# Two cuts of x moved one product ahead, and another first transfer on ScalarE's queue

## The chip, the cores and the metric

The kernel runs on one core of one Trainium2 chip. The metric is the device time of one execution in microseconds (us), as the median of the runs shown. A profiled execution gives, beside its own time, the trace that is read below.

## The reference

One encoder layer works on 512 tokens of width 1024, all in float32:

```python
x = x + FFN_RES * _swiglu(_rmsnorm(x, norm_ffn1[l]), w_ffn1_gu[l], w_ffn1_down[l])
h = _rmsnorm(x, norm_mix[l])
xr, gr, q, k, v, ga, gb = jnp.split(h @ w_in[l], splits, axis=-1)
...
x = x + y @ w_out[l]
x = x + FFN_RES * _swiglu(_rmsnorm(x, norm_ffn2[l]), w_ffn2_gu[l], w_ffn2_down[l])
```

`_swiglu` multiplies by a 1024 x 5632 matrix, takes silu of the first half of the columns times the second half, and multiplies by a 2816 x 1024 matrix. Between the two feed-forward networks stand a gated recurrence and a neighbourhood attention. The change touches the first feed-forward network (FFN) alone, and in it the first product, and one small scaling of a constant later on.

## The kernel before, in words

**Precision.** Every float32 operand that TensorE multiplies is split in two: a high part H, made by a copy on ScalarE (`split`, L140), and a low part L, the rest, made by a subtraction on VectorE (L143). A product is then three matmuls: H by H, L by H and H by L. In the rows that follow `wh` and `wl` are the parts of a weight, `xh` and `xl` those of x. A weight's tile is 128 x 1024 and is cut into four pairs of buffers in turn, so the cut of one tile waits until TensorE is done with the tile four before it.

**The lead.** x arrives in eight tiles of 128 x 512, two to a `pair` tile. With each goes a tile of the first weight `w1gu` (`wraw`), the plain part of the first FFN's columns. All of these transfers are issued on SyncE's queue, but for the first weight tile, which is issued on ScalarE's queue (L457), behind `small`, a 128 x 114 tile of constants (L123). For each x tile ScalarE makes the high part scaled by a column of `small` (L191), the square (L197, L200) and a copy scaled by the norm's weight, `xg` (L670).

**The Strassen stage.** The other columns of the first FFN go by one level of Strassen's scheme, in five units of 512 columns of each half (`strassen`, a variant of it with seven products). The seven products of a unit are called `a11`, `a12`, `s1`, `s2`, `s4`, `s3` and `a22` after the form of x that each takes: quarters of x, or one of four sums of quarters. Those sums, the *forms* s1, s2, s4 and s3, are made once and used by all units: `raw` makes each out of `xg` on VectorE (L258 and L256, in halves of 128 x 256), and `cut` splits it in H and L (128 x 512 tiles named `s` in the rows). Each form has two such tiles, so two cuts. `need(n)` in `strassen` says where in the program form n is cut: before, `need("s4")` stands behind product s2, and `need("s3")` behind product s4. A product is 24 matmuls of 128 x 512, in two halves of twelve; each half has one tile of weights and one tile of the form.

**Sums of weights.** Four of a unit's seven products take sums of weight blocks. Some are made by VectorE (`sums`, L340: `pair` plus a `PT` or `wraw` tile, 128 x 1024), some by a transfer that adds (`add`, L335, on GpSimd's queue). Product a11 of unit one, the second unit, is begun early, between s1 and the rest of unit zero. Its later product s1 takes `pair` + `PT`, two sums on VectorE (`pair_523 + PT_735` and `pair_525 + PT_737`).

**What sets the order.** Each engine runs its instructions in one order, fixed when the kernel is built. A scheduler forms it from the program's order, priorities and expected readiness; `after(i, prev)` holds i behind prev in that order without a wait on the chip. So a step that waits holds back all that is queued behind it on its engine. `ready` (L506 to L515) prepares the plain part's hidden tiles (`pre`) once the first norm is known, `plus` (L353) adds a product to a kept one, `put` (L374, L376) makes and turns a hidden tile, and `evict` (L348) copies a product out.

Of the kernel before, what the change touches and what calls it, by code (L numbers as in the profile page):

```python
# [11 lines left out]
AF = mybir.ActivationFunctionType  # L12
ALU = mybir.AluOpType
# [10 lines left out]
HD = 64  # L24
# [19 lines left out]
C_QN, C_KN = 112, 113  # L44
# [42 lines left out]
def block_kernel(ctx: ExitStack, tc, a, out):  # L87
    nc = tc.nc
# [12 lines left out]
    mark = {}  # L101
# [18 lines left out]


    small = const.tile([P, NSMALL], F32, name="small")
    nc.scalar.dma_start(small, a["small"])  # L123
    xd = dram.tile([KT, P, T], F32, name="xd")
    vd = [dram.tile([ROWS, GW, T], F32, name=nm("vd")) for _ in range(2)]
    xres = [None] * KT
# [2 lines left out]
    ones = const.tile([P, P], F32, name="ones")  # L129
# [2 lines left out]
    for _ in range(NWARM):  # L132
        nc.tensor.matmul(aux_t()[:, :P], ones, ones, start=True, stop=True)
    warm = const.tile([P, 1], F32, name="warm")
    nc.scalar.activation(warm, ones[:, 0:1], AF.Sqrt)


    def split(raw, H, L, act=True):
# [42 lines left out]
    def make_xg(gcol, tag):  # L181
        xh, xl = [], []
        for k in range(KT):
            xh.append(xpool.tile([P, T], F32R, tag=f"xh{k}", name=nm("xh")))
            xl.append(xpool.tile([P, T], F32R, tag=f"xl{k}", name=nm("xl")))
        ssum = xpool.tile([P, T], F32, tag="ssum", name=nm("ssum"))

        def one(k):
            g = small[:, gcol + k : gcol + k + 1]
            x = xres[k]  # L190
            nc.scalar.activation(xh[k], x, AF.Copy, scale=g)  # L191
            return nc.vector.scalar_tensor_tensor(xl[k], x, g, xh[k].bitcast(F32), ALU.mult, ALU.subtract)

        def square(k):
            x = xres[k]
            if k == 0:
                nc.scalar.activation(ssum, x, AF.Square)  # L197
            else:
                sq = big_t(n="xsq")
                nc.scalar.activation(sq, x, AF.Square)  # L200
                nc.vector.tensor_tensor(ssum, ssum, sq, ALU.add)

        return xh, xl, ssum, one, square
# [88 lines left out]
    def strassen(src, units, A, norm, hd, need, ready, finish, early):  # L292

        half = T // 2
        prev, out, state_, rc = {}, [], {}, []
# [41 lines left out]
        def sums(ts, os):  # L337
            def one(t, o):
                with nullcontext() if state_["u"] < 2 and early else tc.high_priority():
                    nc.vector.tensor_tensor(t, t, o, ALU.add)  # L340
                return operand(t)
            return [lambda t=t, o=o: one(t, o) for t, o in zip(ts, os)]

# [49 lines left out]
        for u in range(units):  # L393
# [26 lines left out]
            if prev:  # L420
                last_product(prev)
                last_put(prev)
            w = sums(a_, b_)
            product(Z, w, "s2", False, False)
            add(u, a_, 2)
            u2 = evict(Z, "u2")
            if u == 0:
                need("s4")
            product(X, operands(b_), "s4", False, True)
            if u == 0:  # L430
                need("s3")
                ready(rc[0])
                s1 = gate(p1, 0)
            plus(u2, X)
# [9 lines left out]
    def ffn(wgu, ws, wd, xh, xl, forms, ssum, plain, res, emit_out, lead=None, end=None):  # L444
# [7 lines left out]
        if lead is not None:  # L452
            pre = [aux_t() for _ in range(NCB)]
            for k in range(KT):
                lead[0](k)
                raw, H, L = big_t(n="wraw"), big_t(F32R, n="wh"), big_t(F32R, n="wl")
                tc.keep_in_program_order((nc.scalar if k == 0 else nc.sync).dma_start(raw, wgu[k]))  # L457
                if k == 0:
                    cast = nc.vector.tensor_copy(H, raw)
                    after(lead[1](k), cast)  # L460
# [10 lines left out]
            for ps in pre:  # L471
                t = big_t(n="pre")
# [31 lines left out]
        def ready(rc):  # L504
# [4 lines left out]
            for tb, t in enumerate(toks):  # L509
                g, u = t[:, :half], t[:, half:]  # L510
                nc.scalar.activation(g, g, AF.Silu, scale=rc[:, tb : tb + 1])
                after(nc.vector.scalar_tensor_tensor(u, u, neg[:, tb : tb + 1], g, ALU.mult, ALU.mult), mark["cut", "s4"])
                nc.vector.transpose(
                    g.rearrange("p (c f i) -> p f c i", c=NCB, i=32), u.rearrange("p (f c i) -> p f c i", c=NCB, i=32))
                hold(nc.sync.dma_start(hp[tb], g.rearrange("p (c x) -> p c x", c=NCB)))  # L515
# [185 lines left out]

    def lead(k):
        tc.keep_in_program_order(nc.sync.dma_start(xres[k], a["x"][k]))

    nxt = {}

# [38 lines left out]
    sn8 = const.tile([P, 16], F32, name="sn8")  # L745
    nc.vector.tensor_scalar(sn8, sp, -8.0, None, ALU.mult)
    gq8 = const.tile([P, 1], F32, name="gq8")
    nc.vector.tensor_scalar(gq8, small[:, C_QN : C_QN + 1], HD**-0.5, None, ALU.mult)
    gk = small[:, C_KN : C_KN + 1]

    state = {}
# [531 lines left out]
```

## Time and profile before

| | |
|---|---|
| median of 3 runs | 1095.75 us |
| lowest run | 1095.27 us |
| the profiled execution's own time | 1095.27 us |
| its span, first to last instruction | 1093.5 us |
| TensorE matmuls, busy | 1079.7 us, 99% of the span |
| VectorE, busy | 771.2 us, 71% |
| ScalarE, busy | 561.9 us, 51% |
| granted TensorE clock, mean | 0.997 |

Times in the rows are microseconds from the start of the span. A row of the timeline has start, duration, engine, line, operation, the tile written and those read, a count, and in brackets the idle time ahead of it with what ended it. PE is TensorE, PEld its weight load, DVE VectorE, ACT ScalarE, POOL GpSimd; `SPq` and `ACTq` rows are the issue of transfers on SyncE's and ScalarE's queues. Matmuls are pipelined: a row's 0.39 us is one matmul's time in the engine, and the next one starts about 0.23 us after it. A table by stretches has for each engine the busy time with the count of instructions, then the granted clock, the share of the transfer engines and their GB/s. The median run lies 0.48 us above the profiled one.

### The profile page before, as it was taken

To read this page: it belongs to the slowest core of one execution; us is meant where nothing else is said; L and a number is where in the kernel's file an instruction comes from. 1 tells how busy PE (TensorE), PEld (TensorE's weight loads), DVE (VectorE), ACT (ScalarE), POOL (GpSimd) and SP (SyncE) were. 2 spreads that over 40 slices of the span, in tenths; PEclk is the share of its full clock that TensorE was granted. 3 is DMA by queue.
4 is the path that set the end of the run, shared out by engine and by line. 5 is a ranking of instruction groups with operands and counts; after the bars stand their busy time and mean duration, and the time that the engine had idled before them with its cause. 6 is when DMAs were issued, how large, how long until landed. Compare 5 with 4: busy or idle time off the path is not lost.

```text
span 1093.5 us, 14407 instructions
## 1 busy us (share of the span) xinstructions
PE 1079.7 (99%) x5121; PEld 885.9 (81%) x5121; DVE 771.2 (71%) x1222; ACT 561.9 (51%) x866; POOL 198.0 (18%) x340
## 2 busy tenths in 40 slices
PE   9989999999999999999999999999999999999998
PEld 7868888888888778788877788888888888888887
DVE  7788788775327786999868896768677887765322
ACT  7745555553215768876444643356455555544320
POOL 0101012432000342331335232000000001332000
PEclk9999999999999999999999999999999999999999
DMA  9867766785224576582778566564476776676222
GB/s 366 177 198 193 208 176 164 210 258 170 97 83 145 170 230 172 164 224 95 225 223 230 169 220 218 155 230 172 102 197 182 184 201 167 172 256 196 97 75 78
DMA packets 67465, 198.18 MB, mean 181 GB/s; under 512 B 11073, under 2 KB 12865, under 8 KB 67393
## 3 DMA queue, kind: packets, MB, share of 16 engines
q1 hardware_dynamic: 46592, 136.60, 37.0%
q0 software_dynamic: 20512, 60.34, 24.7%
q8 instruction: 40, 0.66, 0.2%
q10 hardware_dynamic: 288, 0.32, 0.1%
q14 instruction: 33, 0.26, 0.1%
HBM read 162.06 MB, written 26.74 MB: 173 GB/s over the span
## 4 chain that ended last, share of the span: by engine, by line
PE 89%; DVE 2%; DMA 1%; ACT 1%; issue 0%; ACTq 0%; DVEq 0%
PE acc L317 18%; PE aux L317 13%; PE acc L167 10%; PE acc L168 10%; PE acc L169 10%; PE acc L899 4%; PE acc L900 4%; PE acc L901 4%; PE aux L169 4%; PE aux L168 4%; PE aux L167 4%; PE aux L1081 1%; PE aux L810 1%; DMA vd<-v 1%; PE aux L1018 1%; DVE wl L143 1%
## 5 line engine op out<-in xcount | busy, mean ns | idle before, releaser
L143 DVE TENSOR_TENSOR wl<-wraw,wh 128x1024 fp32r<-128x1024 f32 (+2 forms) x147 | 169.0, 1151 | 153.1 <-ACT wh L140 150.0
L140 ACT ACTIVATE wh<-wraw 128x1024 fp32r<-128x1024 f32 (+2 forms) x135 | 134.5, 998 | 216.9 <-PE acc L168 157.1
L143 DVE TENSOR_TENSOR wl<-pair,wh 128x1024 fp32r<-128x1024 f32 x80 | 97.6, 1223 | 44.1 <-ACT wh L140 43.8
L140 ACT ACTIVATE wh<-pair 128x1024 fp32r<-128x1024 f32 x80 | 84.8, 1061 | 76.4 <-PE aux L317 54.6
L167 PE MATMUL acc<-xh,wh 128*128 128x512 f32 x288 | 114.4, 397 | 0.0
L169 PE MATMUL acc<-xh,wl 128*128 128x512 f32 x288 | 112.9, 392 | 0.0
L168 PE MATMUL acc<-xl,wh 128*128 128x512 f32 x288 | 112.9, 392 | 0.0
L317 PE MATMUL aux<-wh,s 128*128 128x512 f32 x320 | 100.3, 394 | 3.2 <-ACT s L140 2.0
L317 PE MATMUL acc<-wh,s 128*128 128x512 f32 x320 | 98.6, 390 | 0.0
L899 PE MATMUL acc<-wh,xh 128*128 128x512 f32 x192 | 75.8, 395 | 0.0
L900 PE MATMUL acc<-wh,xl 128*128 128x512 f32 x192 | 74.9, 390 | 0.0
L901 PE MATMUL acc<-wl,xh 128*128 128x512 f32 x192 | 74.8, 390 | 0.0
L317 PEld LDWEIGHTS aux<-wh,s 128*128 128x128 f32 x320 | 60.7, 190 | 17.3 <-ACT s L140 2.4
L317 PEld LDWEIGHTS acc<-wh,s 128*128 128x128 f32 x320 | 60.1, 188 | 12.5
L168 PE MATMUL aux<-hl,wh 128*128 128x512 f32 (+1 forms) x179 | 69.4, 388 | 0.0
L169 PE MATMUL aux<-hh,wl 128*128 128x512 f32 (+1 forms) x179 | 69.4, 388 | 0.0
L167 PE MATMUL aux<-hh,wh 128*128 128x512 f32 (+1 forms) x179 | 69.1, 388 | 0.0
L169 PE MATMUL acc<-hh,wl 128*128 128x512 f32 (+1 forms) x176 | 68.2, 388 | 0.0
L168 PE MATMUL acc<-hl,wh 128*128 128x512 f32 (+1 forms) x176 | 68.2, 388 | 0.0
L167 PE MATMUL acc<-hh,wh 128*128 128x512 f32 (+1 forms) x176 | 68.1, 388 | 0.0
L167 PEld LDWEIGHTS acc<-xh,wh 128*128 128x128 f32 x288 | 54.4, 189 | 13.1 <-issue 2.3
L140 ACT ACTIVATE wh<-PT 128x1024 fp32r<-128x1024 f32 x40 | 42.3, 1060 | 42.3 <-PE acc L317 32.0
(230 smaller groups left out, 2429.3 us busy)
## 6 DMA issues: line engine op xcount, KB each, us to landing
wraw<-wqkv SPq DMA_DIRECT2D x24, 512.0 KB, 4.1
wraw<-wg SPq DMA_DIRECT2D x24, 512.0 KB, 7.0
wraw<-w1d SPq DMA_DIRECT2D x22, 512.0 KB, 3.6
wraw<-w2d SPq DMA_DIRECT2D x22, 512.0 KB, 3.4
PT<-w1s SPq DMA_DIRECT2D x20, 512.0 KB, 6.1
hT<-hd POOLq DMA_DIRECT2D x80, 128.0 KB, 4.1
PT<-w2s SPq DMA_DIRECT2D x20, 512.0 KB, 3.8
hd<-ht SPq DMA_DIRECT2D x32, 256.0 KB, 5.9
```

The costliest lines, as they stand in the source:

```text
L140: mark["H"] = nc.scalar.activation(H, raw, AF.Copy)
L143: return nc.vector.tensor_tensor(L, raw, H.bitcast(F32), ALU.subtract)
L167: nc.tensor.matmul(ps, wh, xh, start=first, stop=False, skip_group_check=skip)
L168: nc.tensor.matmul(ps, wh, xl, start=False, stop=False, skip_group_check=skip)
L169: mark["mm"] = nc.tensor.matmul(ps, wl, xh, start=False, stop=last, skip_group_check=skip)
L317: mark["mm"] = nc.tensor.matmul(pss[tb], x_[:, s], w_[:, c], start=first and k == 0 and x_ is xh_ and w_ is H, stop=k == 3 and w_ is L, sk ...
L810: prev, mm = mm, nc.tensor.matmul(ps[d][b], W[w][o, c], X[x][o], start=x == 1, stop=w + x == 0)
L899: nc.tensor.matmul(pss[j], xh[kk][:, tj], H[:, s], start=kk == 0, stop=False)
L900: nc.tensor.matmul(pss[j], xl[kk][:, tj], H[:, s], start=False, stop=False)
L901: mark["mm"] = nc.tensor.matmul(pss[j], xh[kk][:, tj], L[:, s], start=False, stop=kk == KT - 1)
L1018: mm = hold(nc.tensor.matmul(ps[hp][:, cs], q_[o, n * P : (n + 1) * P], keys(k_[o]), start=k_ is kl, stop=q_ is ql))
L1081: mm = nc.tensor.matmul(pv[h2 * HD : (h2 + 1) * HD, n * P : (n + 1) * P], vt[:, (fi * 2 + h2) * HD : (fi * 2 + h2 + 1) * HD], PT[:, q], st ...
```

## The change

In the first FFN's unit zero, `need("s4")` moves ahead of product s2 and `need("s3")` ahead of product s4. Unit one's weight sums on VectorE are held behind the last cut of form s3. VectorE's step of `ready` is held behind the same cut instead of that of s4. At the start, the transfer of `small` leaves ScalarE's queue and is issued on SyncE's, between the first and the second x tile, so the first weight tile's transfer is the first thing that ScalarE issues; the warm-up activation comes behind that. The first square is held behind the first scaled copy, and a scaling of one column of `small` (`gq8`) is held behind a later step.

```diff
     small = const.tile([P, NSMALL], F32, name="small")
-    nc.scalar.dma_start(small, a["small"])
...
     warm = const.tile([P, 1], F32, name="warm")
-    nc.scalar.activation(warm, ones[:, 0:1], AF.Sqrt)
...
-            nc.scalar.activation(xh[k], x, AF.Copy, scale=g)
+            mark["xh"] = nc.scalar.activation(xh[k], x, AF.Copy, scale=g)
...
             if k == 0:
-                nc.scalar.activation(ssum, x, AF.Square)
+                after(nc.scalar.activation(ssum, x, AF.Square), mark["xh"])
...
                 with nullcontext() if state_["u"] < 2 and early else tc.high_priority():
-                    nc.vector.tensor_tensor(t, t, o, ALU.add)
+                    i = nc.vector.tensor_tensor(t, t, o, ALU.add)
+                    if state_["u"] == 1 and early:
+                        after(i, mark["cut", "s3"])
                 return operand(t)
...
             w = sums(a_, b_)
+            if u == 0:
+                need("s4")
             product(Z, w, "s2", False, False)
             add(u, a_, 2)
             u2 = evict(Z, "u2")
             if u == 0:
-                need("s4")
+                need("s3")
             product(X, operands(b_), "s4", False, True)
             if u == 0:
-                need("s3")
                 ready(rc[0])
                 s1 = gate(p1, 0)
...
-                tc.keep_in_program_order((nc.scalar if k == 0 else nc.sync).dma_start(raw, wgu[k]))
+                ld = (nc.scalar if k == 0 else nc.sync).dma_start(raw, wgu[k])
+                tc.keep_in_program_order(ld)
+                if k == 0:
+                    after(nc.scalar.activation(warm, ones[:, 0:1], AF.Sqrt), ld)
...
-                after(nc.vector.scalar_tensor_tensor(u, u, neg[:, tb : tb + 1], g, ALU.mult, ALU.mult), mark["cut", "s4"])
+                after(nc.vector.scalar_tensor_tensor(u, u, neg[:, tb : tb + 1], g, ALU.mult, ALU.mult), mark["cut", "s3"])
...
     def lead(k):
         tc.keep_in_program_order(nc.sync.dma_start(xres[k], a["x"][k]))
+        if k == 0:
+            tc.keep_in_program_order(nc.sync.dma_start(small, a["small"]))
...
-    nc.vector.tensor_scalar(gq8, small[:, C_QN : C_QN + 1], HD**-0.5, None, ALU.mult)
+    after(nc.vector.tensor_scalar(gq8, small[:, C_QN : C_QN + 1], HD**-0.5, None, ALU.mult), mark["h"])
```

The first place is VectorE around the end of product s2 of unit zero. Before, `s_146` and `s_149` are the two sums of form s4 and `s_148` and `s_151` the low parts of their cuts; `wl_584` belongs to product s2, `wl_620` and `wl_636` to s4, `wl_696` and `wl_712` to s3, and `pair_525` is unit one's second weight sum:

```order
L143 TENSOR_TENSOR wl_584<-pair_367,wh_583 128x1024
L143 TENSOR_TENSOR wl_620<-wraw_415,wh_619 128x1024
L143 TENSOR_TENSOR wl_636<-wraw_417,wh_635 128x1024
L143 TENSOR_TENSOR wl_696<-PT_411,wh_695 128x1024
L256 SCALAR_TENSOR_TENSOR s_146_605<-s_67_257,xg_253 128x256
L256 SCALAR_TENSOR_TENSOR s_146_605<-s_67_257,xg_283 128x256
L143 TENSOR_TENSOR wl_712<-PT_413,wh_711 128x1024
L143 TENSOR_TENSOR s_148_609<-s_146_605,s_147_608 128x512
L256 SCALAR_TENSOR_TENSOR s_149_612<-s_79_315,xg_311 128x256
L256 SCALAR_TENSOR_TENSOR s_149_612<-s_79_315,xg_341 128x256
L340 TENSOR_TENSOR pair_525<-pair_525,PT_737 128x1024
L143 TENSOR_TENSOR s_151_616<-s_149_612,s_150_615 128x512
```

In the changed kernel the same place reads as follows. `s_140` and `s_143` are the sums of form s4, `s_142` and `s_145` their low parts; `s_152` is the first sum of form s3; `wl_598`, `wl_634`, `wl_650` and `wl_696` are the weights of s2, s4, s4 and s3:

```order
L141 TENSOR_TENSOR wl_598<-pair_367,wh_597 128x1024
L141 TENSOR_TENSOR wl_634<-wraw_415,wh_633 128x1024
L254 SCALAR_TENSOR_TENSOR s_140_565<-s_67_257,xg_253 128x256
L254 SCALAR_TENSOR_TENSOR s_140_565<-s_67_257,xg_283 128x256
L141 TENSOR_TENSOR wl_650<-wraw_417,wh_649 128x1024
L141 TENSOR_TENSOR s_142_569<-s_140_565,s_141_568 128x512
L254 SCALAR_TENSOR_TENSOR s_143_572<-s_79_315,xg_311 128x256
L254 SCALAR_TENSOR_TENSOR s_143_572<-s_79_315,xg_341 128x256
L141 TENSOR_TENSOR wl_696<-PT_411,wh_695 128x1024
L141 TENSOR_TENSOR s_145_576<-s_143_572,s_144_575 128x512
L256 TENSOR_TENSOR s_152_619<-xg_149 128x256
L256 TENSOR_TENSOR s_152_619<-xg_175 128x256
```

Both sums of form s4 stand ahead of product s3's weights now, and no sum of unit one's weights stands among them.

The second place is VectorE where unit one's products a12 and s1 follow. Before, `p_128` and `p_129` are the additions of product s3 to a kept product, `wl_746` and `wl_762` the weights of a12, and `wl_787` and `wl_804` those of s1:

```order
L353 TENSOR_TENSOR p_128_519<-p_128_519,acc_369 128x512
L353 TENSOR_TENSOR p_129_520<-p_129_520,acc_370 128x512
L143 TENSOR_TENSOR wl_746<-PT_731,wh_745 128x1024
L143 TENSOR_TENSOR wl_762<-PT_733,wh_761 128x1024
L143 TENSOR_TENSOR wl_787<-pair_523,wh_786 128x1024
L143 TENSOR_TENSOR wl_804<-pair_525,wh_803 128x1024
```

The same place in the changed kernel, where `pair_523` and `pair_525` are the two weight sums of unit one and `p_138` and `p_139` the additions of product a12:

```order
L353 TENSOR_TENSOR p_128_519<-p_128_519,acc_369 128x512
L353 TENSOR_TENSOR p_129_520<-p_129_520,acc_370 128x512
L141 TENSOR_TENSOR wl_762<-PT_733,wh_761 128x1024
L338 TENSOR_TENSOR pair_523<-pair_523,PT_735 128x1024
L338 TENSOR_TENSOR pair_525<-pair_525,PT_737 128x1024
L353 TENSOR_TENSOR p_138_561<-p_138_561,aux_743 128x512
L353 TENSOR_TENSOR p_139_562<-p_139_562,aux_744 128x512
L141 TENSOR_TENSOR wl_787<-pair_523,wh_786 128x1024
L141 TENSOR_TENSOR wl_804<-pair_525,wh_803 128x1024
```

The two sums and a12's two additions stand between the weights of a12 and those of s1; `wl_746` has gone to an earlier place, right ahead of form s3's last cut, behind which come the steps of `ready` and `put`.

The third place is the head of ScalarE's queue. Before:

```order
L123 DMA small<-small 128x114
L135 ACT_TABLE_LOAD
L135 ACTIVATE warm<-ones 128x1
L457 DMA wraw_140<-w1gu 128x512
L191 ACTIVATE xh_108<-pair_125,small 128x512
L197 ACTIVATE ssum_124<-pair_125 128x512
L191 ACTIVATE xh_110<-pair_125,small 128x512
```

And in the changed kernel:

```order
L458 DMA wraw_139<-w1gu 128x512
L461 ACT_TABLE_LOAD
L461 ACTIVATE warm<-ones 128x1
L189 ACTIVATE xh_106<-pair_123,small 128x512
L195 ACTIVATE ssum_122<-pair_123 128x512
L674 ACTIVATE xg_149<-pair_123,small 128x512
L189 ACTIVATE xh_108<-pair_123,small 128x512
```

`small` has left the queue (on SyncE's it stands between the first two x tiles), and the first scaled copy `xg` stands ahead of the second high part.

## The prediction

> **What bounds the kernel now.** I read the page's busy times first, then TensorE's waits, then a table by stretches around them, and last the timeline at each wait.
>
> ```profile
> PE 1079.7 (99%) x5121; PEld 885.9 (81%) x5121; DVE 771.2 (71%) x1222; ACT 561.9 (51%) x866; POOL 198.0 (18%) x340
> ...
> PE aux L317 <- ACT s L140: 2.0, 1, 2.0
> ...
> PE aux L317 <- DVE wl L143: 1.4, 1, 1.4
> PE aux L317 <- DVE s L143: 1.1, 1, 1.1
> ...
> PE aux L468 <- DVE wh L459: 0.8, 1, 0.8
> ```
>
> TensorE is busy nearly throughout, so a change can win only what TensorE waits. Four of its waits lie in the first 80 us, where the change is. The table by stretches says what they cost:
>
> ```profile
> 5.60:50.20 44.60, 44.60 (x200) 37.04 (x201) 36.65 (x54) 36.68 (x59) 5.45 (x6) 1.00 0.90 286
> 55.65:66.76 11.11, 7.90 (x26) 5.52 (x26) 7.30 (x15) 4.38 (x7) 0.88 (x1) 0.85 0.73 231
> 72.20:84.85 12.65, 11.21 (x50) 8.94 (x48) 12.51 (x14) 5.35 (x6) 0.00 (x0) 1.00 0.59 193
> 84.85:215.57 130.72, 130.72 (x578) 108.33 (x577) 101.88 (x109) 70.26 (x86) 25.04 (x36) 1.00 0.72 187
> ```
>
> ```profile
> 85.01 10.88 PE acc L317 x48
> ```
>
> The last row, from the chain of waits, gives TensorE's pace when nothing holds it: 10.88 us for 48 matmuls, so 0.227 us each and 5.44 us for a product of 24. From 5.60 to 50.20 us, and from 84.85 us on, it never idles. In the second stretch stand the 24 matmuls of unit zero's product s4: 11.11 us where 5.44 are needed, 5.67 lost. In the third stand unit one's a12 and s1: 12.65 against 10.88, 1.77 lost. The timeline shows by what:
>
> ```profile
> 46.46 1.22 DVE L340 TENSOR_TENSOR pair<-pair,wraw 128x1024 f32<-128x1024 f32 x1
> 48.87 1.22 DVE L143 TENSOR_TENSOR wl<-pair,wh 128x1024 fp32r<-128x1024 f32 x1
> 50.01 2.54 DVE L143 TENSOR_TENSOR wl<-wraw,wh 128x1024 fp32r<-128x1024 f32 x2
> 52.95 1.06 ACT L140 ACTIVATE wh<-PT 128x1024 fp32r<-128x1024 f32 x1 [1.17 <-issue]
> 54.05 1.22 DVE L143 TENSOR_TENSOR wl<-PT,wh 128x1024 fp32r<-128x1024 f32 x1 [1.49 <-ACT wh L140]
> 55.19 0.75 DVE L256 SCALAR_TENSOR_TENSOR s<-s,xg 128x256 f32<-128x256 f32 x2
> 57.09 0.63 ACT L140 ACTIVATE s<-s 128x512 fp32r<-128x512 f32 x1
> 57.77 1.35 PE L317 MATMUL aux<-wh,s 128*128 128x512 f32 x3 [1.96 <-ACT s L140]
> 57.89 0.68 DVE L143 TENSOR_TENSOR s<-s,s 128x512 fp32r<-128x512 f32 x1
> 62.25 1.22 DVE L340 TENSOR_TENSOR pair<-pair,PT 128x1024 f32<-128x1024 f32 x1 [3.01 <-DMA PT<-w1s]
> 64.13 0.50 PE L317 MATMUL aux<-wh,s 128*128 128x512 f32 x1 [1.13 <-DVE s L143]
> ```
>
> Product s4 waits for its form twice. The first time the form's sum (55.19) stands behind the low part of a later product's weight (54.05), whose high part could not be cut before TensorE was half through s2 (52.95). The second time VectorE sits 3.01 us on unit one's weight sum (62.25), whose transfer has not landed, with the form's low part queued behind. Between the two, TensorE runs at half clock:
>
> ```profile
> 60.00:61.00 1.00, 1.00 (x4) 0.81 (x3) 0.00 (x0) 0.00 (x0) 0.00 (x0) 0.50 1.04 426
> ...
> 74.00:75.00 1.00, 0.17 (x1) 0.00 (x0) 1.00 (x2) 0.00 (x0) 0.00 (x0) 1.00 0.85 326
> ```
>
> The granted clock of 0.85 over the 11.11 us of the second stretch is 1.67 us of the 5.67. The clock halved after the wait of 1.96 us and a broken start, and did not after the wait of 1.44 us at 74 to 75.6 us.
>
> The third loss is VectorE's backlog behind the late form:
>
> ```profile
> 64.66 0.88 DVE L512 SCALAR_TENSOR_TENSOR pre<-pre,nrc 128x256 f32<-128x256 f32 x2
> ...
> 66.73 0.77 DVE L513 STREAM_TRANSPOSE pre<-pre 128x256 f32<-128x256 f32 x2
> ...
> 69.46 1.25 DVE L353 TENSOR_TENSOR u<-u,aux 128x512 f32<-128x512 f32 x2
> ...
> 70.64 1.40 DVE L374 SCALAR_TENSOR_TENSOR u<-u,rcol,s 128x512 f32<-128x512 f32 x2
> ...
> 71.95 1.30 DVE L376 STREAM_TRANSPOSE ht<-u 128x512 f32<-128x512 f32 x2
> ...
> 73.17 1.25 DVE L353 TENSOR_TENSOR p<-p,acc 128x512 f32<-128x512 f32 x2
> 74.34 2.35 DVE L143 TENSOR_TENSOR wl<-PT,wh 128x1024 fp32r<-128x1024 f32 x2
> 75.61 0.74 PE L317 MATMUL aux<-wl,xh 128*128 128x512 f32 x2 [1.44 <-DVE wl L143]
> ```
>
> **The forms moved ahead.** I lay the new order out with these durations, on the clock of before; a VectorE step that follows another directly starts about 0.08 us before the row of the other ends, as 69.46 + 1.25 and 70.64 show. VectorE: weight sum 46.46, wl of s2 48.87, first wl of s4 50.01 to 51.2; then s4's first sum to 51.9, second wl of s4 to 53.0 (its high part is ready, or the pair at 50.01 would have waited), low part of the form's first tile to 53.6, second sum to 54.3, s3's weight to 55.4, low part of the second tile to 56.0. ScalarE's two casts (0.63 each) fall in its gaps, at 51.9 and 54.3. TensorE ends s2 at 55.65, wants the first tile then and the second at 58.37. Both are there, with 2.0 and 2.4 us to spare. Product s4 runs 55.65 to 61.09, with no half clock. The 5.67 us are gone.
>
> Form s3 is late next: its sums and low parts follow at 56.0 to 59.2 on VectorE, around s3's second weight (0.75, 1.22, 0.68, 0.75). Then a12's first weight must wait until TensorE is half through s4, at 58.4; its cast takes 1.06, its low part runs 59.5 to 60.7, and the last low part of s3 is done at 61.3. Product s3 wants its tiles at 61.09 and 63.81: the first is there at 58.6, the second at 61.3. It runs until 66.53, and unit one's a12, whose first weight is cut, half way on to 69.25.
>
> On VectorE the rest is one chain from 61.2: the steps of `ready` (two rows of 0.88, two of 0.77, 3.0 with the overlaps) to 64.2, then 1.18, 1.31, 1.22 and 1.17 from the starts of 69.46 to 74.34, to 69.07. Now a12's second weight: ready 70.3. Four matmuls can go without it, so TensorE wants it at 69.25 + 0.91 = 70.16: **0.2 lost**, and a12 ends at 72.15. The sum for s1's first weight ends at 71.4, its cast (1.06) at 72.5: **0.4 lost**. Four matmuls later, at 73.5, TensorE wants its low part; but the second sum (to 72.5), a12's two additions (to 73.6) and then the low part itself come first, ready at 74.9: **1.4 lost**. After that VectorE leads again: s1's second low part is due at 77.4 and ready at 76.0, and a22's first low part, due at 79.9, is ready at 77.1. Product a22 begins at 79.4, where it began at 84.85, the end of the third stretch. Of 7.44 us lost, 2.0 stay: **5.4 us won**. The moved GpSimd transfers (the additions into the two PT tiles, now at 71.4 and 72.5) are wanted no sooner than unit one's s3, 16 us after a22's start; SyncE's queue gets one PT load ahead of `ready`'s stores, and nobody waits for those here.
>
> **The start.**
>
> ```profile
> 0.74 0.41 ACTq L123 DMA_DIRECT2D small<-small  x1
> 0.74 0.87 SPq L703 DMA_DIRECT2D pair<-x  x2
> ...
> 1.25 0.40 ACTq L457 DMA_DIRECT2D wraw<-w1gu  x1
> ...
> 3.85 0.72 ACT L191 ACTIVATE xh<-pair,small 128x512 fp32r<-128x512 f32 x1 [1.17 <-DMA small<-small]
> ...
> 5.03 0.43 DVE L459 CAST wh<-wraw 128x512 fp32r<-128x512 f32 x1 [1.03 <-DMA wraw<-w1gu]
> ...
> 5.60 0.94 PE L468 MATMUL aux<-wh,xh 128*128 128x512 f32 x3 [0.78 <-DVE wh L459]
> ```
>
> ```profile
> wraw<-w1gu SPq DMA_DIRECT2D x7, 256.0 KB, 5.0
> ```
>
> The weight tile took 3.78 us from issue to use; issued at 0.74 it is there at 4.5 and cast by 4.95. `small` took 3.11; issued behind one x tile (0.44 for an issue) at 1.18 it is there at 4.3, and the high part of x is made by 5.0. TensorE starts at about 5.15 instead of 5.60: **0.45 won**. Bounds: `small` behind x as slow as the median weight tile (5.0) gives 6.2 for it and 6.95 for TensorE, 1.35 lost; `small` at 3.85 as before gives 4.95 by the weight's cast, 0.65 won. I take 3.11 because it is `small`'s own. The later x tiles are issued 0.44 later and ScalarE's chain starts 0.45 later, but it has room: from 5.60 to 50.20 us it is busy 36.68 us, TensorE all of the 44.60. The swapped `xg`, the warm-up and `gq8` (0.15, VectorE idle there) cost nothing beside that.
>
> Sum against the profiled 1095.27: less 5.4 and 0.45 is **1089.4 us**. The median of the runs shown is 0.48 above that execution.
>
> **The rivals.**
>
> *Half clock again.* The waits of 0.4 and 1.4 us lie within 2.7 us, between 72.15 and 74.9. The trace has one halving after 1.96 us and a broken start, and none after 1.44. If these two waits together suffice, it costs the 1.67 of before: 1091.1 us, 15%. The Trainium skill (TensorE: Matmul & The Clock Gate, Part 1 and "Why this matters for your kernels") says that a free-running window of about 3.4 us decides and that gaps under some 3 us are safe. By that rule neither kernel halves its clock; the trace of before, with its wait of 1.96 us, does not agree with the 3 us.
>
> *`small` late*, by the bound above: 1.8 us more, 1091.2 us, 10%. For it: it is behind 256 KB. Against it: x's own 256 KB were there by 3.85.
>
> *No new wait at s1*, if VectorE's chain is 1.5 us quicker than the rows: 1087.4, 7%. Against it: the rows are this kernel's own.
>
> *Slower, by a late PT tile.* Unit one's second sum still needs its tile:
>
> ```profile
> 55.30 3.03 SPq L301 DMA_DIRECT2D PT<-w1s  x2
> ```
>
> It was issued at 55.30, behind a `wraw` load that waits for s4's second low part (now 0.5 us later), and the sum began at 62.25, 6.95 us after. The sum now stands at 71.3, so 9 us of slack cover it. Past 71.3, each us of lateness costs one, since a12's additions, s1's and a22's low parts are queued behind. It decides from 71.3 + 5.85 = 77.2 on; landing at 80 it would give 1098 us. It needs a transfer of 22 us: 3%. That some other wait takes back most of the gain, 1094 us, I give 5%. That the order is not what was meant cannot be: it is fixed when the kernel is built.
>
> **How the numbers follow.** The forecast has 60% and its own range 1088.5 to 1090.5. The range given, 1087.2 to 1092.9, goes from no new wait and the best start (1089.4 - 2.0 - 0.2) to half clock and late `small` together (1089.4 + 1.7 + 1.8); it leaves out the last two cases, 8%, and a little at its ends. Two per cent, about what a measurement of this kernel can tell from no change, is 21.9 us; all cases lie within it, so 98% for the same.
>
> **What would show it.** TensorE's waits for `s` at 57 and 64 us gone, the clock at 1.00 there; first matmul near 5.15; a22's first matmul near 79; one wait of some 1.4 us for `wl` at 73 us. Wrong: a wait on `s` in s3, or on `pair` from a transfer.

## The result, and the profile after

The changed kernel took 1086.38 us (median of six runs, 1086.2 to 1090.26), the kernel before 1095.8 us in the same comparison: a ratio of 0.9925, with a 95% interval of 0.9906 to 0.9944. One of the six runs of before, which is also among the three of the table above, took 6211.45 us for a reason that no trace shows; without it the median of before is 1095.75 us. The gain of 0.75% is less than the 2% from which a kernel counts as faster here. The forecast was 1089.4 us, its range 1087.2 to 1092.9: four of the six runs, and so the median, lie up to 1 us below that range. The profiled execution took 1086.2 us, the fastest of the six, with a span of 1084.4 us, where before took 1095.27 and 1093.5: 9.07 us less, where 5.85 were forecast.

TensorE's waits in the changed kernel (in total, how often, the longest):

```profile
PE aux L1024 <- DVE kl L1003: 1.8, 1, 1.8
PE aux L315 <- DVE wl L141: 1.1, 1, 1.1
PE aux L132 <- DVE pol L741: 1.1, 1, 1.1
PE aux L472 <- ACT xh L189: 0.5, 1, 0.5
PE aux L315 <- ACT wh L138: 0.2, 1, 0.2
```

Both waits for `s` are gone, and with them the one for `ql` (1.7 us before, far behind the change). The table by stretches of the changed kernel shows products s4 and s3 without a gap and at full clock, and 1.27 us of idle time behind them:

```profile
55.00:60.40 5.40, 5.40 (x26) 4.46 (x25) 5.33 (x10) 4.75 (x8) 0.00 (x0) 1.00 0.95 346
60.40:66.00 5.60, 5.60 (x26) 4.64 (x25) 5.60 (x14) 1.58 (x3) 0.00 (x0) 1.00 0.64 228
66.00:80.00 14.00, 12.73 (x54) 9.55 (x53) 14.00 (x16) 6.45 (x8) 1.74 (x2) 1.00 0.72 175
```

The timeline of TensorE in the changed kernel, with the first matmuls of s4 (55.36), a12 (66.24), s1 (72.32) and a22 (79.29):

```profile
55.36 0.61 PE L315 MATMUL aux<-wh,s 128*128 128x512 f32 x2
...
66.24 0.39 PE L315 MATMUL aux<-wh,xh 128*128 128x512 f32 x1
...
72.32 1.19 PE L315 MATMUL aux<-wh,s 128*128 128x512 f32 x4 [0.17 <-ACT wh L138]
74.61 0.73 PE L315 MATMUL aux<-wl,s 128*128 128x512 f32 x2 [1.10 <-DVE wl L141]
...
79.29 0.39 PE L315 MATMUL acc<-wh,xh 128*128 128x512 f32 x1
```

From 55.36 to 66.24 are 10.88 us, two products at TensorE's own pace. From 66.24 to 79.29 are 13.05, that is 2.17 more than two products; the forecast had 2.0. VectorE's timeline shows why, at the place that the forecast named: the second weight of a12 (68.74), unit one's two sums (69.87), a12's two additions (72.14), and only then the low part that TensorE waits for (the first of four that begin at 73.33):

```profile
68.74 1.21 DVE L141 TENSOR_TENSOR wl<-PT,wh 128x1024 fp32r<-128x1024 f32 x1
69.87 2.35 DVE L338 TENSOR_TENSOR pair<-pair,PT 128x1024 f32<-128x1024 f32 x2
72.14 1.28 DVE L353 TENSOR_TENSOR p<-p,aux 128x512 f32<-128x512 f32 x2
73.33 4.64 DVE L141 TENSOR_TENSOR wl<-pair,wh 128x1024 fp32r<-128x1024 f32 x4
```

At the start of the changed kernel `small`, issued at 1.20 on SyncE's queue, is there at 4.53, and TensorE begins at 5.30:

```profile
1.20 0.42 SPq L709 DMA_DIRECT2D small<-small  x1
...
4.53 0.72 ACT L189 ACTIVATE xh<-pair,small 128x512 fp32r<-128x512 f32 x1 [1.85 <-DMA small<-small]
...
5.30 1.19 PE L472 MATMUL aux<-wh,xh 128*128 128x512 f32 x4 [0.46 <-ACT xh L189]
```

By a22 the change has won 84.85 - 79.29 = 5.56 us. The other 3.5 us of the 9.07 come in two later places, where the program is the same in both kernels: behind a22 every engine has the same instructions in the same order, but for the scaling `gq8`. One is the wait for `ql` in the kernel before. Four transfers of `vd` are issued from 540.79 on; ScalarE waits for them until 551.40, and so makes the part that `ql` needs late:

```profile
540.79 4.37 SPq L928 DMA_DIRECT2D vd<-v  x4
```

```profile
551.40 0.51 ACT L1045 ACTIVATE p<-so,nmx 128x256 f32<-128x256 f32 x1 [4.85 <-DMA vd<-v]
```

```profile
553.42 0.44 PE L1081 MATMUL aux<-PT,va 128*64 128x128 f32 x4 [1.73 <-DVE ql L994]
```

In the changed kernel TensorE is busy through that whole stretch. The other place is the clock. Both kernels wait for `kl` near 600 us, 1.9 us and 1.8 us. In the kernel before the clock halved behind that wait; 5 us at 0.66 are 1.7 us lost:

```profile
500.00:590.00 90.00, 88.27 (x510) 71.90 (x509) 74.55 (x192) 47.15 (x104) 25.65 (x44) 1.00 0.66 201
...
605.00:610.00 5.00, 5.00 (x29) 4.26 (x26) 3.53 (x23) 4.97 (x16) 0.56 (x1) 0.66 0.56 170
```

In the changed kernel it did not:

```profile
500.00:590.00 90.00, 90.00 (x515) 72.69 (x514) 73.94 (x192) 45.17 (x99) 32.64 (x53) 1.00 0.72 214
590.00:615.00 25.00, 23.19 (x163) 18.56 (x162) 21.84 (x56) 12.70 (x27) 5.98 (x10) 1.00 0.48 148
```

5.56, 1.73 and 1.70 make 8.99 of the 9.07. The question for the experiments was which of this the change does, and which comes and goes with the run.

### The profile page after: what moved, and what is told of

The parts are those of the page before. It is cut to its first block, busy times and chain, and to the rows that moved or that the text cites. A ratio compares the mean times of both kernels' runs of the same rounds, so it can differ in the third digit from the quotient of the medians.

```text
span 1084.4 us, 14405 instructions
## 1 busy us (share of the span) xinstructions
PE 1076.1 (99%) x5121; PEld 883.1 (81%) x5121; DVE 770.8 (71%) x1222; ACT 562.1 (52%) x866; POOL 199.6 (18%) x340
## 4 chain that ended last, share of the span: by engine, by line
PE 95%; DVE 3%; issue 1%; DMA 1%; ACT 1%; SPq 0%; DVEq 0%; ACTq 0%
PE acc L315 19%; PE aux L315 14%; PE acc L165 10%; PE acc L166 10%; PE acc L167 10%; PE acc L905 4%; PE acc L906 4%; PE acc L907 4%; PE aux L166 4%; PE aux L167 4%; PE aux L165 4%; PE aux L1087 1%; PE aux L816 1%; PE aux L1024 1%; DVE wl L141 1%; PE aux L472 1%
## 5 line engine op out<-in xcount | busy, mean ns | idle before, releaser
L167 PEld LDWEIGHTS acc<-xh,wl 128*128 128x128 f32 x288 | 54.1, 188 | 11.5 <-issue 0.4
```

The source lines that it names most:

```text
L167: mark["mm"] = nc.tensor.matmul(ps, wl, xh, start=False, stop=last, skip_group_check=skip)
```

## The experiments

All times are in us. "Before" is the kernel before, run on the same chip in the same comparison.

| kernel | median (lowest to highest, runs) | ratio to before, 95% interval | before |
|---|---|---|---|
| forms alone | 1089.57 (1088.83 to 1091.48, 6) | 0.9962, 0.9948 to 0.9976 | 1094.21 |
| start alone | 1095.92 (1092.09 to 1097.62, 12) | 1.0014, 1.0003 to 1.0024 | 1094.21 |
| no hold | 1086.84 (1085.39 to 1087.78, 6) | 0.9932, 0.9919 to 0.9945 | 1094.21 |
| filled gap | 1086.58 (1086.11 to 1087.13, 6) | 0.9931, 0.9917 to 0.9944 | 1094.21 |
| steady before | 1094.1 (1091.76 to 1095.16, 12) | 0.9991, 0.998 to 1.0003 | 1094.24 |
| steady after | 1087.2 (1086.61 to 1087.84, 5) | 0.9935, 0.9921 to 0.995 | 1094.24 |
| steady, no hold | 1084.82 (1084.26 to 1085.88, 5) | 0.9919, 0.9902 to 0.9935 | 1094.24 |
| filled gap, shorter warm-up | 1087.54 (1085.95 to 1088.41, 5) | 0.9937, 0.9921 to 0.9952 | 1094.24 |
| steady, forms alone | 1087.23 (1086.61 to 1088.14, 5) | 0.9938, 0.9926 to 0.9951 | 1094.11 |
| changed kernel again | 1087.03 (1086.54 to 1088.92, 5) | 0.9941, 0.9928 to 0.9953 | 1094.11 |
| `small` on GpSimd's queue | 1088.62 (1087.18 to 1090.38, 5) | 0.9952, 0.9938 to 0.9966 | 1094.11 |
| steady, hold alone | 1091.35 (1089.21 to 1092.18, 8) | 0.9971, 0.996 to 0.9982 | 1094.11 |

**The two parts, each alone.** The first kernel is the changed one with the old start, so it has the hold of unit one's sums too; the second is the kernel before with the new start.

Forms alone, against the changed kernel:

```diff
     small = const.tile([P, NSMALL], F32, name="small")
+    nc.scalar.dma_start(small, a["small"])
...
     warm = const.tile([P, 1], F32, name="warm")
+    nc.scalar.activation(warm, ones[:, 0:1], AF.Sqrt)
...
-                after(nc.scalar.activation(ssum, x, AF.Square), mark["xh"])
+                nc.scalar.activation(ssum, x, AF.Square)
...
-        if k == 0:
-            tc.keep_in_program_order(nc.sync.dma_start(small, a["small"]))
```

> The kernel before with the cuts of s4 and s3 moved ahead and unit one's sums held; the start is the old one. Theory A (three separate sources: the forms' waits, the start, and a late part near 550 and 605 us that differs from run to run): first matmul at 5.6 us, unit one's a22 begins 5.2 to 5.3 us earlier than before (84.85), near 79.6; the best runs at 1086.5, others up to 4 us above, where the wait at 550 us and the half clock at 605 us come back. Rival B (the late part of 3.5 us belongs to the new start): 1090 in all runs.

Start alone, against the changed kernel:

```diff
-                    if state_["u"] == 1 and early:
-                        after(i, mark["cut", "s3"])
...
-            if u == 0:
-                need("s4")
             product(Z, w, "s2", False, False)
...
             if u == 0:
-                need("s3")
+                need("s4")
             product(X, operands(b_), "s4", False, True)
             if u == 0:
+                need("s3")
                 ready(rc[0])
```

> The kernel before with the new start alone. Theory A: first matmul at 5.30, a22's first matmul at 84.5, and 0.3 us off the time of before; runs spread by the same late part, 1091 to 1096. Rival B: 1091.5 in all runs, with the wait at 550 us gone. Rival C (the start's 0.3 us is lost again behind a transfer in the first 50 us): no difference at 50 us.

By the medians the forms alone won 4.6 us and the start alone lost 1.7. So the gain is the forms'; but the two do not add up to the whole, 4.6 - 1.7 = 2.9 against the 9.4 of the whole change. In the trace of the forms alone both waits for `s` are gone and those for `wl` (1.1) and `wh` (0.2) are as in the changed kernel. But a22 begins at 81.77 and not near the expected 79.6, because TensorE's first matmuls follow each other at 0.43 us instead of 0.23, eleven of them from 5.58 to 10.20, though the clock column says 1.00 there. Behind a22 there is a wait of 1.1 us for `ql`, and behind the wait for `kl` the clock halves. TensorE's timeline and two stretches of the forms alone:

```profile
5.58 1.62 PE L472 MATMUL aux<-wh,xh 128*128 128x512 f32 x3 [0.73 <-ACT xh L191]
6.99 1.48 PE L473 MATMUL aux<-wh,xl 128*128 128x512 f32 x3
```

```profile
600.00:605.00 5.00, 4.82 (x35) 4.46 (x36) 3.55 (x17) 4.96 (x12) 0.56 (x1) 0.66 0.66 191
```

```profile
5.58:10.20 4.62, 4.62 (x11) 3.65 (x12) 4.62 (x8) 4.62 (x9) 0.00 (x0) 1.00 1.05 397
```

In the trace of the start alone a22 begins at 88.39, where 84.5 was expected. VectorE's second sum for unit one waited 4.26 us for its PT tile, until 8.2 us after SyncE began to issue the two PT loads at 55.66. TensorE waited 4.0 us for `s` behind it, where the profile of before had 1.1, and the half clock that followed lasted 6.83 us and not 3.41:

```profile
63.86 1.23 DVE L338 TENSOR_TENSOR pair<-pair,PT 128x1024 f32<-128x1024 f32 x1 [4.26 <-DMA PT<-w1s]
```

Nine of its twelve runs had a mean granted clock of 0.996 or less, against one of the 17 runs of before. So in the old order the new start may itself bring more half clock; the runs don't show why.

Three things vary from run to run by more than the start could win: the landing of that PT tile (as long as the form's cut stands behind it), the clock after the wait for `kl`, and the clock of the first matmuls.

**The hold.** Is the hold of unit one's sums behind form s3's last cut needed, and does it make the waits at a12 and s1? Against the changed kernel:

```diff
                     i = nc.vector.tensor_tensor(t, t, o, ALU.add)
-                    if state_["u"] == 1 and early:
-                        after(i, mark["cut", "s3"])
```

> The changed kernel without the rule that holds unit one's weight sums behind the last cut of s3. In VectorE's order one sum then stands ahead of s2's second weight, where VectorE waits anyway, and the other behind s1's first low part. Theory A: the wait of 1.1 us for wl near 73 us goes, a22 begins 1.1 to 1.3 us earlier, 1085.0. Rival D (the hold is what frees form s4): s4 waits again, 2 us and more lost at 56 us.

1086.84 us, the same as the changed kernel. Its trace is better where the edit is: no wait for `wl` or `wh`, and the waits for `s` stay away. TensorE's waits, without the hold:

```profile
PE aux L1022 <- DVE kl L1001: 1.8, 1, 1.8
PE aux L132 <- DVE pol L739: 1.1, 1, 1.1
PE aux L1085 <- DVE ql L998: 1.0, 1, 1.0
```

The last of them is the wait for `ql`, and behind that for `kl` the clock halved:

```profile
597.00:600.00 3.00, 3.00 (x20) 2.72 (x17) 1.82 (x13) 2.97 (x8) 0.56 (x1) 0.51 0.74 255
```

What the edit won, those two took. In this kernel the runs don't sort by the clock: four with 0.998 took 1085.39 to 1086.99 us, two with 0.999 took 1086.77 and 1087.78. A comparison of a few tenths of a per cent needed them out of the way.

**The gap for `kl` filled.** Four matmuls of `ones` by `ones` into a buffer that is written anew right behind, in the changed kernel, ahead of the scores that wait for `kl`. They add work and change no output:

```diff
+            if hf == 1 and fi == 0:
+                for _ in range(4):
+                    hold(nc.tensor.matmul(pss[n2s[0]][1][:, :P], ones, ones, start=True, stop=True))
             for n in [n2 * 2 + i for n2 in n2s for i in range(2)]:
```

> The changed kernel with four extra matmuls of ones by ones (128x128) ahead of the second half's first scores, in the gap of 1.8 us near 595 us in which TensorE waits for kl; they add work and change no result. Theory A (the half clock after that gap comes or not by where the gap falls against the clock's window): with the gap filled the half clock never follows, all runs at a clock of 0.999 or more after that place, best run still 1086.2, and the upper runs fall by up to 1.7 us. Rival E (the upper runs come from waits on transfers): the spread of 4 us stays. If the gap isn't there, the four cost up to 1.9 us.

The fill took the first half of the wait, and 0.9 us of it stayed. TensorE's timeline with the gap filled:

```profile
595.03 1.05 PE L1016 MATMUL aux<-ones 128*128 128x128 f32 x8
597.01 0.39 PE L1027 MATMUL aux<-kl,qh 64*128 64x256 f32 x2 [0.92 <-DVE kl L1003]
```

The median is that of the changed kernel, but the six runs lie within 1.0 us of each other, where the changed kernel's spread over 4.1, and every one had a granted clock of at least 0.999. So the wait for `kl`, when it is 1.8 us long, is what halves the clock in some runs of the changed kernel, and 0.9 us does not do it. One stretch of half clock costs 1.7 us; the changed kernel's two runs with 0.998 were 3 to 4 us above its others, and what made up the rest isn't shown, as neither was traced.

**Both kernels steadied.** Now before and after with the fill, and with one more warm-up matmul at the start, against the half clock of the first products; and the third likewise without the hold. Against each kernel, beside the lines of the fill:

```diff
-NWARM = 8
+NWARM = 9
```

> The kernel before, with the four extra matmuls in the gap near 600 us and nine warm-up matmuls in place of eight, so that the gap between the warm-up and the first product shrinks from 0.75 to about 0.3 us. Theory F (the clock is granted at the end of a window of about 3.4 us only if TensorE idles in little of it, and taken back after a window in which it idles much, and where the windows lie differs from run to run): no half clock in the first 12 us and none at 605 us; what stays is the change's sure part, the two waits for s and the half clock between them, 1092 to 1094. Rival G (the clock at the start does not hang on the warm-up): half clock for up to 4.6 us at the start in some run, spread as before.

> The changed kernel with the same two edits. Theory F: all runs within 1 us of 1086.2, and 6 us or more below the kernel before with these edits: the part of the gain that does not hang on the clock's windows (0.3 from the start, 5.3 from the forms, of it 1.7 half clock). Rival G: as without the ninth warm-up matmul, 1086.1 to 1087.1, since its first product had no half clock in the profile shown.

> The changed kernel with the same two edits and without the hold on unit one's weight sums. The wait of 1.1 us for wl at 73 us is gone as in the profile without the hold, and so are the half clocks: 1084.9. If the waits at 550 us are larger in it by chance of its order, up to 1086.

The two edits did not steady the kernel before: its median is that of before (0.9991, interval 0.998 to 1.0003), and its runs spread over 3.4 us. Steady before and steady after differ by 6.9 us in the medians. In the profiled executions a22 begins at 87.48 and 79.31, and the totals are 1094.37 and 1086.66: 8.17 us by a22, 7.71 at the end; the difference is a wait of 0.4 us for `ql` in the steady after. The gain now is all ahead of a22. It is larger than the 5.56 of the first two profiles mainly because the PT tile was late again; 0.7 us are slow first matmuls of the steady before. TensorE's waits for `s` in it:

```profile
PE aux L317 <- DVE s L143: 3.4, 1, 3.4
PE aux L317 <- ACT s L140: 2.0, 1, 2.0
```

Steadied and without the hold the kernel took 1084.82 us, 2.4 less than the steady after, and less than both kernels of this case. In its profile a22 begins at 77.29, 2.02 us sooner than in the steady after, and the list of TensorE's waits has only two:

```profile
PE aux L132 <- DVE pol L739: 1.1, 1, 1.1
PE aux L1025 <- DVE kl L1001: 0.9, 1, 0.9
```

So with the forms moved ahead the hold costs its 2 us, and form s4 is in time without it. VectorE makes unit one's two sums at 47.90 and at 71.17 us there: one before the forms' cuts and one behind them, so neither keeps TensorE from a form.

**A shorter warm-up.** Does a longer idle time ahead of the first product bring the half clock there? The kernel with the filled gap, one warm-up matmul fewer:

```diff
-NWARM = 8
+NWARM = 7
```

> The changed kernel with the four extra matmuls in the gap near 595 us and only seven warm-up matmuls, so the gap ahead of the first product grows from about 0.4 to 0.9 us. Theory F: a window that holds the gap no longer grants the clock, so most runs begin with 1 to 4.6 us of half clock: median 0.5 to 2 us above that with eight (1086.6). Rival G: no difference, or 0.1 us.

In its trace it did not: with 0.93 us idle ahead of it the first product ran at its full pace, where in the forms alone, with 0.73 us idle, it ran at half. So the length of that gap alone isn't what decides; the last section shows what does. The median, 1087.54 us, can't be told from that of the filled gap with eight (1086.58), since the intervals of the two ratios overlap.

**The start, steadied.** The forms alone again, with the fill and nine warm-up matmuls; beside it the changed kernel once more, unedited.

```diff
-NWARM = 8
+NWARM = 9
...
+                for _ in range(4):
+                    hold(nc.tensor.matmul(pss[n2s[0]][1][:, :P], ones, ones, start=True, stop=True))
```

> The forms moved ahead and unit one's sums held, with the old start, and the two edits that steady the clock (four extra matmuls in the gap near 595 us, nine warm-up matmuls). Against the changed kernel with the same edits (1087.2) it tells the start's worth. Theory A: 0.3 to 0.5 us more, 1087.6, and a22's first matmul near 79.7. Rival H (the old start also leaves TensorE at half clock in its first 5 us, as in the profile of the forms alone): 1089 and more, a22 2 us later.

> The changed kernel once more, unedited, beside the others on one chip. Theory A: runs in two groups, near 1086.5 with a clock of 0.999 or more and 1.7 us and more above it with 0.998, since the gap of 1.8 us near 595 us stays open; median 1086.3 to 1088.5. Rival (the four extra matmuls changed nothing): all runs within 1 us as in those kernels.

With the old start 1087.23 us and a ratio of 0.9938, with the new one 1087.2 and 0.9935: no difference that can be measured. Its first matmuls ran at full pace this time, though they began at 5.57, where those of the forms alone began at 5.58. TensorE's timeline, old start, steadied:

```profile
5.57 0.93 PE L472 MATMUL aux<-wh,xh 128*128 128x512 f32 x3 [0.83 <-DVE wh L463]
6.33 0.86 PE L473 MATMUL aux<-wh,xl 128*128 128x512 f32 x3
```

That one more warm-up matmul does this isn't shown: the steady before, which has it too, ran its first three slowly, and the changed kernel, which has it not, ran none slowly.

The changed kernel again took 1087.03 us, a ratio of 0.9941: 7.1 us less than before in this comparison, where the first had 9.4 between the medians. Over its eleven runs here and above, the seven with a granted clock of 0.999 or 1.0 took 1086.2 to 1087.03, the four with 0.998 took 1088.54 to 1090.26.

**`small` on the third queue.** If `small` is what the first product waits for, would a queue of its own be sooner? The kernel without the hold, gap filled, eight warm-up matmuls, with `small` first on GpSimd's queue:

```diff
     small = const.tile([P, NSMALL], F32, name="small")
+    nc.gpsimd.dma_start(small, a["small"])
...
-        if k == 0:
-            tc.keep_in_program_order(nc.sync.dma_start(small, a["small"]))
```

> The changed kernel without the hold on unit one's sums, with the four extra matmuls, and small's transfer first on GpSimd's queue instead of behind the first x tile on SyncE's. Theory: the first product waits for x's high part, which waits for small (4.53); on its own queue it lands near 4.0, the weight's cast is next late (4.28 to 4.71), first matmul near 4.9 instead of 5.3; 1084.5 against 1084.8. Rival: GpSimd's transfer takes longer or x is as late as small: first matmul 5.3 or later, no gain.

No: 1088.62 us, 3.8 more than the steadied kernel without the hold. The timeline has `small` 4.44 us after its issue on GpSimd (1.29 to 5.73), where SyncE's queue took 3.33, and the first matmuls at half pace, four in 2.08 us. Two of its five runs had a granted clock of 0.998 although the gap for `kl` is filled; neither was traced:

```profile
1.29 0.73 POOL L123 DMA_DIRECT2D small<-small  x1 [0.84 <-POOLq L1278]
...
5.73 0.72 ACT L190 ACTIVATE xh<-pair,small 128x512 fp32r<-128x512 f32 x1 [3.05 <-DMA small<-small]
...
6.50 2.08 PE L471 MATMUL aux<-wh,xh 128*128 128x512 f32 x4 [1.66 <-ACT xh L190]
```

In the profiles 1.2 us are the later first matmul, 1.2 the slow ones (by the same product near 28 us the lag is 2.37), and 1.4 a wait for `ql`.

**The hold alone.** The steady before with nothing of the change but the hold, so that the PT tile no longer stands ahead of form s4:

```diff
-                    nc.vector.tensor_tensor(t, t, o, ALU.add)
+                    i = nc.vector.tensor_tensor(t, t, o, ALU.add)
+                    if state_["u"] == 1 and early:
+                        after(i, mark["cut", "s3"])
```

> The kernel before with one part of the change, the hold of unit one's weight sums behind the last cut of s3, and the two steadying edits; the forms stay at their old places. Against the kernel before with those edits (1094.1 median) it tells how much of the gain is the second wait, for a transfer. Theory A: the wait of 2.0 for the first s stays, with half clock after it in most runs; the second wait (1.1 to 3.4) is gone; a22 near 83 instead of 85 to 87.5; 1091 to 1092.5. Rival I (moving the forms is the whole gain): no difference.

1091.35 us, 2.75 less than the steady before (0.2%, 2.2 us, by the two ratios, since the two ran in different comparisons). The second wait for `s`, behind the transfer, is gone; the first stays at 2.0, and a12 waits 1.9 for `wl`. In the trace a22 begins at 82.31, 5.17 us sooner than in the steady before; but the traced run is the fastest of the eight. TensorE's waits and its timeline:

```profile
PE aux L317 <- ACT s L140: 2.0, 1, 2.0
PE aux L317 <- DVE wl L143: 1.9, 1, 1.9
```

```profile
57.80 1.35 PE L317 MATMUL aux<-wh,s 128*128 128x512 f32 x3 [1.96 <-ACT s L140]
...
72.19 0.73 PE L317 MATMUL aux<-wl,xh 128*128 128x512 f32 x2 [1.92 <-DVE wl L143]
```

The rest of the steady gain, 1091.35 - 1087.2 = 4.15 us in the medians, comes with the forms' earlier place (and the new start, which won nothing measurable). Neither of those two waits was followed by a half clock in this trace; five of the eight runs had a granted clock of 0.998, so half clock is part of the median.

## Why the prediction was right, and where it was not

*The forms.* The steps held. Both waits on `s` went and the clock stayed at 1.00 between 55 and 66 us. Form s3 and the PT tile were in time. What is late next is what was named: the low part for s1, behind the two sums and a12's additions. The forecast 2.0 us of new loss measured 2.17 by the distance from a12 to a22, of which 1.27 shows as idle time; the rest is TensorE starting again behind each wait. The wait for `wl` was 1.1 instead of 1.4 us.

*The start.* 0.45 was forecast and 0.30 came, since `small` took 3.33 us and not 3.11. Of these, 0.29 reached s4 (55.36 against 55.65). In the total it can't be measured: with and without it, steadied, the medians differ by 0.03 us. The forecast had no term for the half pace of the first matmuls, which costs up to 2.2 us and was seen with either start.

*By a22* 5.85 us were forecast and 5.56 measured: that was the part that the prediction worked out, and its error is 0.3 us.

*The step that failed* is the sum "against the profiled 1095.27", where the gain up to 84.85 us was passed on to the end with nothing added: "from 84.85 us on, it never idles" had been read from a stretch that ends at 215.57, and it was carried over the other 870 us. There the profile of before held two losses, 1.73 us at 553 and 1.70 at 605, that are not part of the program's steady time and that the profiled execution of the changed kernel did not have. That is why the time fell below the range. How much of such losses falls on a traced execution is luck: between the medians of the second comparison, where the changed kernel ran again, the gain is 7.1 us. The range's low end, made of terms of the changed stage alone, had no room for a difference between executions.

*A term mis-sized* is the second wait for `s`. The prediction took 1.1 us and one half clock (1.67) from its one trace. It is a transfer's landing, and was 1.1, 4.0 and 3.4 us in three traces of the old order; behind the 4.0 the half clock lasted two windows, 3.4 us lost. So the change takes away more than the trace of before showed: 8.17 us by a22 in the steadied pair. In that pair the two later losses of before's first trace were absent, and so the gain in the totals, 7.71 us, was smaller than the 9.07 of the first pair.

*The rivals.* "Half clock again" did not happen: behind 0.2 and 1.1 us the clock was 1.00 in every trace of the changed order. By the last section the forecast's 0.4 and 1.4 us, 1.8 together, would have been just at the limit if both had fallen into one window; the measured waits put at most 1.28 us into one. `small` was not late on SyncE's queue; "no new wait at s1" needed VectorE quicker, and it was not, but the order without the hold gave it. The late PT tile did not matter in the new order: unit one's second sum stood ready behind the cuts.

*Still open:* why the transfer `vd` was late near 550 us in some traces (waits for `ql` of 1.7, 1.4, 1.1, 1.0, 0.5, 0.4, 0.3 us or none); why the start alone had more half clock than before; and whether the hold's and the forms' shares, 2.75 and 4.15 us, add up in this way in other runs, since the steady before itself spread over 3.4 us.

## What to carry to other kernels

Read where a wait ends, and ask if it is a computation or a transfer: here the first was 2.0 us in four traces of the old order, and the second was 1.1 to 4.0 us, so it deserves a range and not a number. When two profiled executions are compared, make the sum at the end of the changed stage as well as at the end of the kernel; what is won later, where the program is the same, belongs to the run. And try an edit that holds steps back without that hold too: here, with the forms moved ahead, it protected nothing and cost 2 us, though alone in the old order it won 2.2 to 2.75.

## What the runs showed of the hardware

Waits of the same length halve the clock in one execution and not in another. After 1.9 us for `kl` the kernel before fell to 0.66 over 5 us, the changed kernel after 1.8 us did not, and without the hold it did again after 1.8 us. After 1.96 us for `s` the clock halved in the profile of before and stayed in that of the hold alone. The traces hold the reason, as each records the moments at which the granted clock changes. In the kernel before, the times between these moments are 54.61, 3.41, 542.72, 3.41 and 484.69 us: 16, 1, 159, 1 and 142 times 3.413 us. In the other thirteen traces they are whole multiples of it too. So the clock is decided in windows of 3.41 us, and where these lie differs from execution to execution. These are the windows ahead of and behind the waits, first those of the kernel before, then those of the changed kernel's wait for `kl` (the second number is the window's length, the third TensorE's busy time, and the third from the end the granted clock):

```profile
55.88:59.29 3.41, 1.40 (x5) 0.88 (x6) 2.56 (x5) 1.85 (x4) 0.00 (x0) 1.00 1.02 299
59.29:62.70 3.41, 3.41 (x10) 2.46 (x8) 0.45 (x1) 0.93 (x2) 0.00 (x0) 0.50 0.94 383
602.01:605.42 3.41, 1.55 (x25) 1.50 (x24) 3.41 (x7) 3.36 (x5) 0.10 (x1) 1.00 0.44 116
605.42:608.84 3.42, 3.42 (x18) 2.89 (x15) 1.95 (x13) 3.41 (x11) 0.56 (x1) 0.50 0.63 180
```

```profile
592.17:595.58 3.41, 2.45 (x23) 1.48 (x19) 1.79 (x4) 1.31 (x3) 1.98 (x3) 1.00 0.47 105
595.58:598.99 3.41, 2.56 (x33) 2.39 (x33) 3.41 (x12) 3.38 (x3) 0.00 (x0) 1.00 0.24 75
```

A wait that falls into one window leaves 1.9 or 2.0 us of it idle, and the next window is at half clock, which costs 1.7 us. The same wait across the border of two windows leaves about 1 us idle in each (0.96 and 0.85 here, and 0.96 and 1.12 for `s` in the hold alone), and nothing follows. Over all fourteen traces, six windows at full clock with 1.81 to 3.04 us idle were followed by half clock, and none with up to 1.78 us was; one with 1.82 us was not either, so the limit lies near 1.8 us. A wait of 0.9 us can't reach it alone. These are the windows of theory F in the expectations above. That the idle time in the window is the cause is read from these traces; no run here sets it.

The Trainium skill (TensorE: Matmul & The Clock Gate, Part 1) says that a free-running window of about 3.4 us of activity decides, so that the phase counts; that fits these rows. Its table in "Why this matters for your kernels" calls gaps of up to about 3 us safe; with the granted clock at 0.66 and 0.51 behind 1.8 and 1.9 us, the traces here do not agree.

The first matmuls of the kernel ran at 0.43 us apart instead of 0.23 in some executions, for up to 4.6 us, while the granted clock was shown as 1.00. That 1.00 is no measurement: the tables show it ahead of a trace's first record of the clock. In the forms alone this record, a change to full clock, stands at 10.37 us; the matmuls are 0.43 us apart up to 10.40 and 0.23 from there. In the five traces with slow first matmuls it stands at 6.01 to 10.37 us, behind the first product's begin, in the nine others at 5.61 or sooner. The window that ends at this record had 0.56 us of idle time or less in every trace. No window ahead of it did: the least had 0.73. So a first matmul is fast when such a busy window ends before it. The same page of the Trainium skill says that the number of slow first matmuls varies from run to run with that window's phase. The traces agree: the forms alone and the kernel before have the same program in their first 5.5 us, and eleven matmuls filled 4.62 us in the one, while in the other none ran at half pace.
